# Start addresses of the matmul operands in SBUF, shifted by padding: a hybrid decoder layer on one core

## The chip, the cores and the metric

One core of a Trainium2 chip runs the kernel. The metric is the device time of one execution in microseconds (us); lower is better. A time shown for a kernel is the median of several executions. Beside it stands one profiled execution, whose trace gives the start and the duration of every instruction on every engine.

## The reference

The reference is one layer of a hybrid decoder on 512 positions with a width of 2048, in float32. What matters here is which matrix products it holds:

```
h    = rms_norm(x, norm1_w)
proj = h @ w_in                       # 2048 -> q, k, v (1024 each), z 1024, x/B/C 1536, dt 16
attn = moba_attention(rms(q), rms(k), v)          # 8 heads x 128, causal
ssm  = ssd_chunked_scan(silu(conv4(xBC)), dt, a)  # 16 heads x 64, state 128, gated by silu(z)
x    = x + concat(attn, ssm) @ w_out  # 2048 -> 2048
u    = conv3(rms_norm(x, norm2_w) @ w_up)         # 2048 -> 11264
y    = x + (silu(u_gate) * u_val) @ w_down        # 5632 -> 2048
```

## The kernel before

**Split operands.** A float32 operand `a` is split into `hi` (rounded to the float32r format, on ScalarE) and `lo = a - hi` (on VectorE). A product is then three float32r matmuls: the two with `hi` weights against both parts of the activations, and `lo` weights against the first part. TensorE holds the stationary operand of 128 x 128, which a weight load brings in, and streams the moving operand past it. Both are read from SBUF.

**First stage** (input projection, attention, scan, output projection). All activations lie in 16 tiles `A0..A15` (hi) and 16 tiles `B0..B15` (lo) of [128, 512]. Weights come by DMA into the ring `raw` (3 tiles of [128, 1024]) and are split into the rings `hi` and `lo` (3 tiles of [128, 528] each) by `issue_split`. There are two forms of use. In the feature-major form (`fm_uses`, `wide_use`, through `mm3`) the weights are stationary and `A[k]`, `B[k]` move, 512 columns at a time: `hi.A`, `hi.B`, `lo.A`. In the token-major form (`tok_use`, for v and z) a 128-column slice of `A[k]` or `B[k]` is stationary and the weights move, with 256, 264 or 512 columns. The attention and scan work is done in generators that a planner (`advance`, `Paced`) sets between the pieces when the program is written; the order of the instructions is then fixed. In this stage nearly all instructions carry line 183, the helper's.

**Second stage** (the two products of the gated MLP). Each is done by a seven-product scheme (Strassen-Winograd): 44 `up` groups and 24 `down` groups, each of the products P1 to P7. A product has 8 (in the `down` passes 7, 8 and 7) slices of 128 rows; each slice is one `hi` weight slice against both parts of an activation tile (lines 1286 and 1287), and then all slices of the `lo` weights (line 1289), 256 columns each: 24 matmuls a product, or 21. `items` fixes the order P5(g), P3(g-1), P1(g), P4(g-1), P6(g), P2(g), P7(g). The weights lie in `hi2` (3 tiles) and `lo2` (2 tiles) of [128, 1024], and the activations in seven tiles `cmb0..cmb6` of [128, 2, 8, 256], one for each product:

```
KT1, KT3, K11, KT2, K21, K22, KT4 = range(7)
KIND = {"P5": KT1, "P7": KT3, "P1": K11, "P6": KT2, "P2": K21, "P3": K22, "P4": KT4}
        pool = p2["cmb"] if t < K22 else p2["cmbl"]
```

So P3 streams `cmb5` and P4 `cmb6`, which lie in the left pool `w2`, and the other five stream `cmb0..cmb4`, which lie in a pool at the right end of SBUF.

**Where tiles lie.** Pools on the left are stacked from address 0 of each partition, those on the right from the end. At the left end lie the DMA descriptor scratch (16384 bytes by default), 128 bytes of constants of the framework, and the pool `consts` (5152 bytes), so that the next pool begins at byte 21664. There the pools `w` (`raw`, `hi`, `lo`) and `ab` (`A`, `B`) lie in the first stage, and, once these are closed, the pool `w2` (`par2` 1408 bytes, `rawb`, `rawa`, `acc_s`, `hi2`, `lo2` of 4096 bytes a tile, then `cmb5`, `cmb6`). Summed up, the start addresses modulo 512 bytes are:

| operand | first byte | modulo 512 |
|---|---|---|
| `hi`, three tiles of 2112 bytes | 33952 | 160, 224, 288 |
| `lo`, three tiles of 2112 bytes | 40288 | 352, 416, 480 |
| `A`, `B`, 32 tiles of 2048 bytes | 46624 | 32 |
| `hi2`, `lo2`, five tiles of 4096 bytes | 55840 | 32 |
| `cmb5`, `cmb6` of 16384 bytes | 76320 | 32 |
| `cmb0` to `cmb4` of 16384 bytes | 147424 | 480 |
| attention's `PTh`, `PTl` and `vh`, `vl` (right pool) | 180192 | 480 |

A weight slice of 128 columns has 512 bytes, a moving slice of 256 or 512 columns 1024 or 2048, so all slices of a tile have the same address modulo 512 (but the second slice of the 264-column pieces, which is 32 bytes further).

Of the kernel before, what the change touches and what calls it, by code (L numbers as in the profile page):

```python
# [20 lines left out]
F32 = mybir.dt.float32  # L21
F32R = mybir.dt.float32r
# [165 lines left out]
def body(ctx, tc, xT, wi, wz, wo, wu, wd0, wd1, wd2, pp, pf, outT, dbg={}):  # L188
    nc = tc.nc
# [9 lines left out]
    wpool = ab.enter_context(tc.tile_pool(name="w", bufs=3))  # L199
    abp = ab.enter_context(tc.tile_pool(name="ab", bufs=1))  # L200
# [9 lines left out]


    RW = 1024
    BEHIND = 2.5
    pieces = []

# [14 lines left out]
    def issue_dma(upto):  # L230
        while state["dma"] <= min(upto, len(raw_q) - 1):
            ci = state["dma"]
            src, width = raw_q[ci]
            r = wpool.tile([128, RW], F32, name="raw")
            if ci == 0:
                nc.sync.dma_start(r[:, :512], src[:, :512])
                nc.sync.dma_start(r[:, 512:width], src[:, 512:])
            else:
                nc.sync.dma_start(r[:, :width], src)
            raws[ci] = r  # L240
            state["dma"] += 1

    def issue_split(upto):
        while state["split"] <= min(upto, len(pieces) - 1):
            i = state["split"]
            ci, o, w, _ = pieces[i]
            issue_dma(ci)
            h = wpool.tile([128, 528], F32R, name="hi")
            l = wpool.tile([128, 528], F32R, name="lo")
            src = raws[ci][:, o:o + w]  # L250
            clk["last"] = ("pe", clk["pe"])
            A_.activation(h[:, :w], src, AF.Copy)
            V.tensor_tensor(l[:, :w], src, h[:, :w].bitcast(F32), op=OP.subtract)
            his[i] = (h, l)
            ready[i] = clk["dve"]
            state["split"] += 1

    def dump(n, ap):
        if n in dbg:
            nc.sync.dma_start(dbg[n], ap)  # L260


    A = [abp.tile([128, S], F32R, name=f"A{k}") for k in range(NK)]
    B = [abp.tile([128, S], F32R, name=f"B{k}") for k in range(NK)]
    C = [cpool.tile([128, S], F32, name=f"C{k}") for k in range(NK)]
# [13 lines left out]
    def pc(name, i=0, n=1):  # L279
        o = _PC[name] + i  # L280
        return (p2["par"] if name[0] == "f" else par)[:, o:o + n]
# [54 lines left out]
    def step(e):  # L336
        clk["last"] = ("pe", clk["pe"])
        old = clk["pe"], clk["act"], clk["dve"], clk["pool"]
        e[3] = 0
        try:  # L340
            say = next(e[0])
        except StopIteration:
            if e in gens:
                gens.remove(e)
            return
        if old != (clk["pe"], clk["act"], clk["dve"], clk["pool"]):
            e[1] = max(clk[k] for k in ("pe", "act", "dve", "pool") if k != "pool" or clk[k] != old[3]) + 0.3
        if e not in gens:
            e[2] = e[2] or say == "soon"
            gens.append(e)  # L350
        elif say == "soon":
            e[2] = True
        elif say == "later":
            e[2] = False

    def advance(force=False):

        for e in list(gens):
            e[3] += 1
            ready_ = clk["pe"] >= e[1]  # L360
            if force or (e[2] and (ready_ or e[3] > 1)) or \
                    (ready_ and max(clk["act"], clk["dve"]) < clk["pe"] + BEHIND):
                step(e)
# [308 lines left out]
    def tok_use(k0, nk, cols, box, done):  # L672

        def use(h, l):
# [5 lines left out]
            for kk, t in order:  # L680
# [3 lines left out]
                o = box["acc"][t][:, :cols]  # L684
                T.matmul(o, A[k][:, ts_], h[:, cc], start=k == 0, stop=False)
                T.matmul(o, A[k][:, ts_], l[:, cc], start=False, stop=False)
                T.matmul(o, B[k][:, ts_], h[:, cc], start=False, stop=k == NK - 1)
# [3 lines left out]

    XR = lambda k: (A[k], B[k])

# [8 lines left out]
    def prep_x(k):  # L702
        t = ssq_box[k]
        A_.activation(A[k], t, AF.Copy, scale=pc("nw1", k))
        V.scalar_tensor_tensor(B[k], t, pc("nw1", k), A[k].bitcast(F32), op0=OP.mult, op1=OP.subtract)

# [131 lines left out]
    def split_mix(i):  # L838
# [5 lines left out]
        dump("mix%d" % k, C[k])  # L844
        A_.activation(A[i], C[k], AF.Copy)
        V.tensor_tensor(B[i], C[k], A[i].bitcast(F32), op=OP.subtract)
# [15 lines left out]
    def cmb_tile(t):  # L862

        pool = p2["cmb"] if t < K22 else p2["cmbl"]
        return pool.tile([128, 2, 8, 256], F32R, name="cmb%d" % t)
# [78 lines left out]
    V.memset(u_t[:, 0:3], 0.0)  # L944
    prep_x(0)
    issue_split(0)
    sq_x(0)
    issue_split(1)
    prep_x(1)
    sq_x(1)  # L950
    prep_x(2)
    issue_split(2)
    sq_x(2)
    mix_at = {}
# [15 lines left out]
    lp = ctx.enter_context(tc.tile_pool(name="w2", bufs=1, reuse_waits="tile"))  # L970
# [150 lines left out]
    def x_load(n):  # L1121
        if n < 4:
            x_ld.append(side_tile(box["pool"], [4, 256], "ld", 3))
            sy.dma_start(x_ld[n], xd[:, 4 * (n % 2):4 * (n % 2) + 4, n // 2, :])

    def x_split(n):
        t, h = (K22, KT4)[n // 2], n % 2
        if h == 0:
            up_kinds[t] = cmb_tile(t)
        o = up_kinds[t][:, :, 4 * h:4 * h + 4, :]  # L1130
        se.activation(o[:, 0], x_ld[n], AF.Copy)
        ve.tensor_tensor(o[:, 1], x_ld[n], o[:, 0].bitcast(F32), op=OP.subtract)
        x_load(n + 3)

    for n, slot in enumerate((2, 4, 5, 6)):
        at(slot, x_split, n)
# [135 lines left out]
    for k, (gi, x) in enumerate(items):  # L1272
# [6 lines left out]
        h, l = parts.pop(k)  # L1279
        bk = g["kinds"][KIND[x]]  # L1280
        n = g["n"]
# [36 lines left out]
```

## Time and profile before

| | |
|---|---|
| median of 3 runs | 2115.16 us (2113.25 to 2115.39) |
| profiled execution | 2114.84 us |
| its span, first to last instruction | 2113.1 us |
| TensorE busy | 2073.9 us (98%), 15366 matmuls |
| VectorE busy | 1583.5 us (75%) |
| ScalarE busy | 988.3 us (47%) |
| mean granted TensorE clock | 0.998 of full speed |

The profiled execution's own time is 1.7 us over its span. Engines work in parallel, and busy times overlap. Matmuls are pipelined: one takes 0.28 or 0.39 us from its start to its end, but the next starts before it ends. The number that counts is the spacing from one start to the next, and TensorE can be busy for all of a stretch in which this spacing is longer than it need be.

### The profile page before, as it was taken

Reading aid. Unit: us, or ns where it says so; the run is one execution under the profiler, and the core shown is the slowest. Engines: PE = TensorE matmul, PEld = TensorE weight load, DVE = VectorE, ACT = ScalarE, POOL = GpSimd, SP = SyncE. Lnnn points to the kernel's source line nnn. Section 1 sums busy time; section 2 is a strip of 40 time slices with the busy share of each in tenths; the row PEclk is TensorE's granted clock in tenths of the full one; section 3 lists DMA queues with packets and bytes.
Section 4 is the critical chain, followed back from the end, with each engine's and each line's share of the span. In section 5 each row is a group of like instructions: output and inputs, shape, how many; then the busy total and the mean of one; then the engine's idle time right before and its main releaser. Section 6 shows DMA issues by size and latency. Waiting matters only on the chain.

```text
span 2113.1 us, 37694 instructions
## 1 busy us (share of the span) xinstructions
PE 2073.9 (98%) x15366; PEld 1949.7 (92%) x15366; DVE 1583.5 (75%) x2251; ACT 988.3 (47%) x1433; POOL 207.9 (10%) x107
## 2 busy tenths in 40 slices
PE   9999999999999998999999999999999899999999
PEld 7888887888888878999999999999999899899999
DVE  6545555345555558999999999999999977977976
ACT  5433435244344435555555555555555534534532
POOL 0020000000000001111110111011111111101110
PEclk9999999999999999999999999999999999999999
DMA  5233222332225535445444444454455667856763
GB/s 194 75 115 91 71 75 76 99 101 80 80 70 172 165 129 188 158 141 189 160 156 165 170 168 155 157 183 158 142 188 201 215 215 242 274 184 231 260 201 120
DMA packets 114396, 328.18 MB, mean 155 GB/s; under 512 B 10736, under 2 KB 35120, under 8 KB 111408
## 3 DMA queue, kind: packets, MB, share of 16 engines
q1 hardware_dynamic: 114224, 325.78, 45.5%
q8 instruction: 120, 1.97, 0.4%
q14 instruction: 52, 0.43, 0.1%
HBM read 283.77 MB, written 41.98 MB: 154 GB/s over the span
## 4 chain that ended last, share of the span: by engine, by line
PE 88%; DVE 7%; issue 2%; ACT 1%; DMA 1%; SPq 0%; DVEq 0%; POOL 0%; ACTq 0%; POOLq 0%
PE acc L183 29%; PE x L1289 16%; PE x L1286 16%; PE x L1287 16%; PE sm L183 4%; PE y L1289 3%; PE y L1287 3%; PE y L1286 3%; DVE lo L1050 2%; DVE cmb L1097 1%; DVE lo L183 1%; DVE acc L1151 0%; DVE s L1024 0%; DMA raw<-wi 0%; DVE s L1030 0%
## 5 line engine op out<-in xcount | busy, mean ns | idle before, releaser
L1287 PE MATMUL x<-cmb,hi 128*128 128x256 f32 x3168 | 755.0, 279 | 12.5 <-DVE cmb L1097 10.9
L1286 PE MATMUL x<-cmb,hi 128*128 128x256 f32 x3168 | 755.8, 279 | 11.5 <-ACT cP L1166 5.4
L1287 PEld LDWEIGHTS x<-cmb,hi 128*128 128x128 f32 x3168 | 599.3, 189 | 15.2 <-DVE cmb L1097 13.4
L1286 PEld LDWEIGHTS x<-cmb,hi 128*128 128x128 f32 x3168 | 598.7, 189 | 13.4 <-issue 7.5
L1289 PE MATMUL x<-cmb,lo 128*128 128x256 f32 x3168 | 434.3, 279 | 2.6 <-DVE lo L1050 2.6
L1289 PEld LDWEIGHTS x<-cmb,lo 128*128 128x128 f32 x3168 | 397.2, 189 | 3.6 <-DVE lo L1050 3.4
L183 DVE TENSOR_TENSOR lo<-raw,hi 128x512 fp32r<-128x512 f32 (+1 forms) x240 | 164.4, 691 | 243.0 <-ACT hi L183 228.5
L1041 ACT ACTIVATE hi<-s 128x1024 fp32r<-128x1024 f32 (+1 forms) x201 | 201.0, 1000 | 287.3 <-DVE s L1024 192.2
L1017 POOL TENSOR_TENSOR rawb<-rawa,rawb 128x1024 f32<-128x1024 f32 (+1 forms) x68 | 169.7, 2496 | 1308.1 <-DVE s L1024 1070.8
L183 PE MATMUL acc<-A,hi 128*128 128x512 f32 x704 | 281.5, 400 | 0.5 <-ACT hi L183 0.5
L183 PE MATMUL acc<-A,lo 128*128 128x512 f32 x704 | 277.9, 395 | 0.1
L183 PE MATMUL acc<-B,hi 128*128 128x512 f32 x704 | 276.8, 393 | 0.0
L183 ACT ACTIVATE hi<-raw 128x512 fp32r<-128x512 f32 (+1 forms) x240 | 149.6, 629 | 256.2 <-PE acc L183 220.3
L1050 DVE TENSOR_TENSOR lo<-s,hi 128x1024 fp32r<-128x1024 f32 (+1 forms) x201 | 238.6, 1187 | 18.8 <-issue 18.8
L1050 DVE TENSOR_TENSOR lo<-rawa,hi 128x1024 fp32r<-128x1024 f32 (+1 forms) x204 | 242.0, 1186 | 3.6 <-PE x L1289 3.6
L1041 ACT ACTIVATE hi<-rawa 128x1024 fp32r<-128x1024 f32 (+1 forms) x204 | 209.5, 1028 | 40.0 <-PE x L1287 39.9
L183 PEld LDWEIGHTS acc<-A,lo 128*128 128x128 f32 x704 | 132.1, 188 | 33.0 <-DVE lo L183 2.1
L183 PEld LDWEIGHTS acc<-A,hi 128*128 128x128 f32 x704 | 132.7, 188 | 29.5 <-ACT hi L183 1.8
L183 PEld LDWEIGHTS acc<-B,hi 128*128 128x128 f32 x704 | 132.5, 188 | 28.3
L1166 ACT ACTIVATE cP<-x 128x256 f32<-128x256 f32 x132 | 50.9, 385 | 214.0 <-PE x L1289 214.0
L183 PE MATMUL acc<-hi,A 128*128 128x256 f32 (+2 forms) x448 | 135.4, 302 | 0.7 <-DVE u L183 0.7
L183 PE MATMUL acc<-lo,A 128*128 128x256 f32 (+2 forms) x448 | 133.5, 298 | 0.0
(204 smaller groups left out, 2777.2 us busy)
## 6 DMA issues: line engine op xcount, KB each, us to landing
rawa<-wu SPq DMA_DIRECT2D x176, 512.0 KB, 3.6
raw<-wi SPq DMA_DIRECT2D x79, 512.0 KB, 3.6
rawa<-wd SPq DMA_DIRECT2D x64, 448.0 KB, 4.1
rawb<-wu SPq DMA_DIRECT2D x44, 512.0 KB, 4.5
gd<-gt SPq DMA_DIRECT2D x22, 1024.0 KB, 4.6
raw<-wo SPq DMA_DIRECT2D x32, 512.0 KB, 3.6
rawa<-wd SPq DMA_DIRECT2D x32, 512.0 KB, 4.4
ld<-gd SPq DMA_DIRECT2D x27, 512.0 KB, 6.4
```

The source lines that it names most:

```text
L183: return fn(out, *args, **kw)
L1017: po.tensor_tensor(r, raw[gi, "11"][:, :n], r, op=OP.subtract)
L1041: se.activation(h[:, :n], src[:, :n], AF.Copy)
L1050: ve.tensor_tensor(l[:, :n], src[:, :n], h[:, :n].bitcast(F32), op=OP.subtract)
L1097: ve.tensor_tensor(lo, ld[:, :m, :], hi.bitcast(F32), op=OP.subtract)
L1166: se.activation(g[x], X[:, 256:] if x == "P5" else X[:, :256], AF.Copy)
L1286: pe.matmul(out, w, bk[:, 0, q, :], start=fresh and q == 0, stop=False, skip_group_check=True)
L1287: pe.matmul(out, w, bk[:, 1, q, :], start=False, stop=False, skip_group_check=True)
L1289: pe.matmul(out, l[:, q * 128:(q + 1) * 128], bk[:, 0, q, :], start=False, stop=q == n - 1, skip_group_check=True)
```

## The change

All tiles on the left lie at other addresses. The width of the ring tiles `hi` and `lo` becomes 640 columns (2560 bytes, a multiple of 512). A tile `space` of 112 columns (448 bytes) that nothing reads or writes lies in front of `A0`, and a like one (`space2`) in front of `cmb5`. The descriptor scratch at address 0 shrinks to 1024 bytes, so that everything behind it starts 15360 bytes (30 x 512) lower. No instruction is added, removed or moved, and no operand's shape changes.

```diff
+    WT = 640
...
-            h = wpool.tile([128, 528], F32R, name="hi")
-            l = wpool.tile([128, 528], F32R, name="lo")
+            h = wpool.tile([128, WT], F32R, name="hi")
+            l = wpool.tile([128, WT], F32R, name="lo")
...
+    abp.tile([128, 112], F32, name="space")
     A = [abp.tile([128, S], F32R, name=f"A{k}") for k in range(NK)]
...
     def x_split(n):
         t, h = (K22, KT4)[n // 2], n % 2
+        if n == 0:
+            lp.tile([128, 112], F32, name="space2")
         if h == 0:
             up_kinds[t] = cmb_tile(t)
...
-    nc = _bacc.Bacc("TRN2", target_bir_lowering=False, num_devices=1)
+    nc = _bacc.Bacc("TRN2", target_bir_lowering=False, num_devices=1, dynamic_dma_scratch_size=1024)
```

## Rows read from the trace of the kernel before

**Rows 1.** The page: busy time of each engine, and its share of the span.

```profile
PE 2073.9 (98%) x15366; PEld 1949.7 (92%) x15366; DVE 1583.5 (75%) x2251; ACT 988.3 (47%) x1433; POOL 207.9 (10%) x107
```

**Rows 2.** Waits of TensorE from 790 us: total us, times, longest us.

```profile
PE x L1287 <- DVE cmb L1097: 10.9, 11, 2.3
```

**Rows 3.** Timeline of TensorE: first matmuls of P5, P3, P1, P4, P6, P2.

```profile
1107.37 0.28 PE L1286 MATMUL x<-cmb,hi 128*128 128x256 f32 x1
...
1110.09 0.28 PE L1286 MATMUL x<-cmb,hi 128*128 128x256 f32 x1
...
1112.95 0.29 PE L1286 MATMUL x<-cmb,hi 128*128 128x256 f32 x1
...
1115.69 0.28 PE L1286 MATMUL x<-cmb,hi 128*128 128x256 f32 x1
...
1118.55 0.29 PE L1286 MATMUL x<-cmb,hi 128*128 128x256 f32 x1
...
1121.29 0.28 PE L1286 MATMUL y<-cmb,hi 128*128 128x256 f32 x1
```

**Rows 4.** Windows: TensorE's busy time, matmuls touched, granted clock, DMA share, GB/s.

```profile
660.00:760.00 100.00, 100.00 (x432) 1.00 0.52 164
390.00:420.00 30.00, 30.00 (x132) 1.00 0.30 91
475.00:490.00 15.00, 15.00 (x130) 1.00 0.25 71
1300.00:1600.00 300.00, 300.00 (x2606) 1.00 0.47 167
```

**Rows 5.** Timeline of TensorE in a down group: first matmuls of P3 and P1.

```profile
1945.78 0.28 PE L1286 MATMUL x<-cmb,hi 128*128 128x256 f32 x1
...
1948.64 0.29 PE L1286 MATMUL x<-cmb,hi 128*128 128x256 f32 x1
```

**Rows 6.** Timeline of TensorE in attention: probabilities against values, 256 columns.

```profile
226.33 0.28 PE L183 MATMUL sm<-PTh,vl 128*128 128x256 f32 x1
...
227.05 0.28 PE L183 MATMUL sm<-PTh,vl 128*128 128x256 f32 x1
```

**Rows 7.** Timeline of TensorE: the third and fifth matmul of P1.

```profile
1113.20 0.28 PE L1286 MATMUL x<-cmb,hi 128*128 128x256 f32 x1
...
1113.43 0.28 PE L1286 MATMUL x<-cmb,hi 128*128 128x256 f32 x1
```

**Rows 8.** Timeline of TensorE: one-column matmuls, each behind a full weight load.

```profile
257.75 1.05 PE L183 MATMUL sm<-ones,t 128*128 128x1 f32 x8 [0.94 <-DVE PTl L183]
258.66 0.36 PE L183 MATMUL acc<-hi,A 128*128 128x256 f32 x1
```

**Rows 9.** Timeline of TensorE in the first stage, feature-major: twelve matmuls apart.

```profile
500.31 0.39 PE L183 MATMUL acc<-B,hi 128*128 128x512 f32 x1
...
503.07 0.39 PE L183 MATMUL acc<-B,hi 128*128 128x512 f32 x1
```

**Rows 10.** Groups of TensorE's instructions by line and shape.

```profile
L183 PE MATMUL acc<-A,hi 128*128 128x512 f32 x704 | 281.5, 400 | 0.5 <-ACT hi L183 0.5
L183 PE MATMUL acc<-hi,A 128*128 128x256 f32 x256 | 73.5, 287 | 0.0
```

**Rows 11.** Timeline of TensorE, token-major: third `lo` tile moving, and the next.

```profile
399.68 0.39 PE L183 MATMUL acc<-lo,A 128*128 128x512 f32 x1
399.92 0.39 PE L183 MATMUL acc<-hi,B 128*128 128x512 f32 x1
```

**Rows 12.** Windows over one group, 1104.65 to 1124.01, summed: busy us of each engine.

```profile
sum 19.36, PE 19.36 PEld 19.36 DVE 18.11 ACT 10.06 POOL 2.46; mean PE 2.77 PEld 2.77 DVE 2.59 ACT 1.44 POOL 0.35
```

**Rows 13.** Waits of all engines in the second stage's steady part, 1000:1600.

```profile
DVE lo L1050 <- PE x L1289: 10.4, 16, 0.7
DVE ug L1172 <- PE x L1289: 7.0, 16, 0.4
```

## The prediction

> **What bounds the kernel now.** I read the page first. TensorE is busy for 2073.9 us of a span of 2113.1, and no other engine for more than 75% [rows 1]. Then TensorE's waits: from 790 us on the longest entry is 10.9 us in 11 waits, for activations at the borders of passes [rows 2]. So the time is a count of matmuls times the spacing of their starts, and the next view is the timeline, to find this spacing. It is not one number. In an up group P5, P3, P1, P4, P6 and P2 begin at 1107.37, 1110.09, 1112.95, 1115.69, 1118.55 and 1121.29 us [rows 3]. P5 takes 2.72 us, 113.3 ns for each of 24 matmuls; P3 and P4 take 2.86 us; P1 and P6, which follow those two, 2.74 us. P2 and P7 together have 5.44 of the group's 19.36 us [rows 12], 2.72 each. The shapes and the clock are the same (1.00 in each window, [rows 4]), and TensorE never stops. A down group, with other work on VectorE and the queues, has the same 2.86 us for P3 [rows 5]. So the length goes with the product and not with what else runs. What P3 and P4 have of their own is where their activations lie: 32 bytes modulo 512, which is what `hi2` and `lo2` have, while the other five products have 480.
>
> I call moving start minus stationary start, modulo 512, the offset. It is 448 (that is, -64) for P1, P2, P5, P6, P7 and 0 for P3 and P4. The rows that bear on it: attention's product of probabilities and values has 480 on both sides, offset 0, and its six matmuls from 226.33 to 227.05 stand 120 ns apart [rows 6], which is P3's settled spacing. There the moving operand starts at 480 too, so 480 by itself is not what makes P5 fast; the offset is. And P1's first two spacings are 0.25 us together, the next two 0.23 [rows 3, 7]: a change of offset takes a few matmuls to settle.
>
> How near 113.3 ns is to the floor: eight one-column matmuls, each behind a full weight load, take 0.91 us [rows 8], 114 ns each, the first one's wait included. The 256-column products at offset -64 are as fast as their weight loads.
>
> In the first stage the spacing is 230 ns for 512 columns (2.76 us for twelve, [rows 9]) and 232 over 100 us of the output projection (100.39 us by 432 matmuls, [rows 4]). There `hi` has offsets 384, 320 and 256 and `lo` 192, 128 and 64, so every matmul is followed by one with another offset, and none has -64.
>
> **The change, part by part.** *Descriptor scratch.* 15360 bytes are 30 x 512: by itself this changes no address modulo 512. It makes the room for the rest. All DMAs of this program are started on SP, and no instruction of it reads or writes the scratch: 0 us.
>
> *`space2` in front of `cmb5`.* `w2` begins at 21664 - 15360 = 6304; with `par2` and 13 tiles of 4096 bytes `cmb5` would begin at 60960, with the padding it does at 61408, which is 480 modulo 512. `hi2` (40480) stays at 32. P3 and P4 get the offset -64 of the other five. If they take 2.72 us, P1 and P6 have nothing to settle either, and a group of 24-matmul products loses 2 x 0.14 + 2 x 0.02 = 0.32 us. 44 up and 8 down groups have 24, 16 down groups 21 (three settled matmuls less, 2 x 0.02 us): 52 x 0.32 + 16 x 0.28 = 21.1 us. The other way to count it: 300.28 us hold 2606 matmuls [rows 4], 115.2 ns, and at 113.3 all 11088 would take 21 us less.
>
> *Rings of 640 columns and `space`.* `hi` starts at 18592, `lo` at 26272, each tile 2560 = 5 x 512 bytes long: all six at 160. They end at 33952, `A0` begins at 34400, and all `A`, `B` are at 96. In the feature-major form the offset is now -64 for every matmul. There are three forms of 704, so 2112, of 512 columns [rows 10]. What that gives is not in the trace, since no long run of 512 columns has one offset. [...] I take 222, nearer to 220 because the steady case of P5 is the like one: 9 ns x 2112 = 19 us. One tenth I take off for places where TensorE will wait for attention and scan work: 17 us.
>
> The token-major form gets offset 64 in every matmul: three forms of 256, so 768, of 256 columns [rows 10], and by the plan in the code 384 of 264 and 192 of 512. Now they take about 118 (15.28 us by 130) and 230 (30.39 us by 132) [rows 4]. Nothing shows a steady 64. If it were like -64: 5 x 1152 + 10 x 192 = 8 us gained; if like 0, 2 x 1152 = 2 us lost. I take 0.
>
> *What could take it back.* VectorE has 18.11 us of work in a group of 19.36 [rows 12], and a group would now take 19.04. Its idle time is in part waiting for TensorE, 17.4 us in 600 in the two longest such waits [rows 13], 0.56 us a group by 31 groups, against 0.32 taken away. It stays covered; with no cover at all the group couldn't go under 18.11. The waits on activations at the pass borders [rows 2] are chains of DMA, ScalarE and VectorE; they keep their length.
>
> [...] The trace shows 2.72 and 2.86 us for equal products [rows 3]. [...]
>
> Sum: 2114.8 (the profiled execution; the median is 0.3 higher) - 21.1 - 17 = 2076.7 us.
>
> **The rivals.**
> - *The second stage alone gains.* At 512 columns the weight load is hidden behind the matmul and the slow part has another cause, as the third `lo` tile hints [rows 11]. Then 2114.8 - 21.1 = 2093.7, with the token-major bounds 2086 to 2096. [...]
> - *The offset modulo 512 is not the cause, but the region.* `cmb0..4` lie over 147000, `hi2` under 69000; all slow pairs lie on one side together (`cmb5` and `hi2` low, `PTh` and `vh` high). If the operands must lie in different halves, the change does not do what it says: P3 and P4 stay at 2.86, the first stage stays slow, 2115 give or take 4. Against it: it would have to be halves of the whole memory, for `cmb6`, 24 KB and more behind `hi2`, is no faster than `cmb5`, 8 KB behind it: P3 and P4 are equal [rows 3].
> - *Slower.* One steady offset locks the 512-column matmuls into a bad relation where now good and bad ones mix. To lose, they must cost more than they do now by 21.1 + 4.2 us by 2304 matmuls, 11 ns each, 242 ns. Single spacings of 0.24 us occur [rows 11], longer runs of them do not. At 245 ns: 2114.8 - 21.1 + 14 x 2304 / 1000 = 2126.
>
> **How the numbers follow.** Both stages gain: 0.62, from 2063 (220 ns, nothing lost, the token-major form like -64: 21.1 + 23.2 + 8 = 52 us) to 2087 (227 ns, 8 us). Second stage alone: 0.23. Region, or nothing: 0.11. Slower: 0.04. The predicted time is the first case's, 2077. The range from 2063 to 2096 takes in the second case and leaves out the third and fourth and a little of the tails. A measurement of this kernel can tell about 0.2% from no change. Faster by more: 0.62 + 0.23 and a little of the third, 0.87; within: 0.09; slower: 0.04.
>
> **What would show it.** Right: P3, P4, P1 and P6 at 2.72 us each, a group at 19.04; twelve feature-major matmuls in 2.64 to 2.70 us instead of 2.76; the stretch of the output projection with more than 440 matmuls in 100 us. Wrong: P3 still at 2.86 (region); first stage at 230 (second stage alone); VectorE's `lo` ending TensorE's waits inside the up groups (cover gone). The step I am least sure of is the 222 ns.

## The result, and the profile after

The changed kernel takes 2130.76 us (median of 6 runs, 2128.54 to 2133.87) against 2113.6 (6 runs): a ratio of 1.0081 (95% interval 1.0068 to 1.0094). It is slower by 17 us where 37 us less had been forecast. The profiled execution took 2133.87 us, its span is 2132.2.

The page of the changed kernel, busy times, answers to [rows 1]:

```profile
PE 2093.8 (98%) x15366; PEld 1967.6 (92%) x15366; DVE 1583.5 (74%) x2251; ACT 988.2 (46%) x1433; POOL 207.8 (10%) x107
```

VectorE and ScalarE did the same work in the same time; TensorE's 15366 matmuls take 20 us more. So it is still a matter of spacings. The timeline of the changed kernel, first matmuls of P5, P3, P1, P4, P6 and P2 of one up group [rows 3]:

```profile
1116.43 0.28 PE L1290 MATMUL x<-cmb,hi 128*128 128x256 f32 x1
...
1119.26 0.28 PE L1290 MATMUL x<-cmb,hi 128*128 128x256 f32 x1
...
1122.09 0.28 PE L1290 MATMUL x<-cmb,hi 128*128 128x256 f32 x1
...
1124.91 0.28 PE L1290 MATMUL x<-cmb,hi 128*128 128x256 f32 x1
...
1127.74 0.28 PE L1290 MATMUL x<-cmb,hi 128*128 128x256 f32 x1
...
1130.57 0.28 PE L1290 MATMUL y<-cmb,hi 128*128 128x256 f32 x1
```

All products are alike now, as forecast, but alike at 2.83 us. P3 and P4 fell from 2.86, and P5, whose operands have the same offset as before, rose from 2.72. Windows of the changed kernel over TensorE (busy time, matmuls touched, granted clock, DMA share, GB/s) [rows 4], two of the first stage and three of the second:

```profile
660.00:760.00 100.00, 100.00 (x430) 1.00 0.52 165
390.00:420.00 30.00, 30.00 (x131) 1.00 0.33 104
900.00:1600.00 700.00, 700.00 (x5946) 1.00 0.46 161
1740.00:1800.00 60.00, 60.00 (x531) 1.00 0.69 226
2020.00:2080.00 60.00, 60.00 (x512) 1.00 0.60 200
```

A window also counts the matmul that was running at its start, so the spacing is taken as its length and the 0.28 us of one matmul, by the count: from 900 to 1600 us 700.28 us by 5946, 117.8 ns. From 1740 to 1800 it is 60.28 by 531, 113.5 ns; from 2020 on 117.7 again. The instructions, the addresses modulo 512 and the clock are the same in the three windows. So one offset has two spacings, and the longer one holds here for hundreds of microseconds. Between two of the windows lies a border of a pass. The timeline of the changed kernel there, one wait and the matmuls behind it:

```profile
1995.28 0.28 PE L1290 MATMUL x<-cmb,hi 128*128 128x256 f32 x1
1997.26 0.38 PE L1291 MATMUL x<-cmb,hi 128*128 128x256 f32 x1 [1.70 <-DVE cmb L1099]
...
1997.60 0.28 PE L1291 MATMUL x<-cmb,hi 128*128 128x256 f32 x1
...
1998.78 0.28 PE L1291 MATMUL x<-cmb,hi 128*128 128x256 f32 x1
```

Behind the wait ten spacings take 1.18 us: the spacing of 117.8 ns has begun. Two shorter waits (0.37 and 0.50 us) in the next 15 us turn it to 113.4 ns for about one product and back.

Where the 19 us of span went: the second stage's first matmul starts at 794.34 us in the timeline of the changed kernel and at 791.31 in that of the kernel before. So the first stage lost 3 us and the second 16.

### The profile page after: what moved, and what is told of

It is laid out like the page before. It is cut to its first block, busy times and chain, and to the rows that moved or that the text cites. A ratio compares the mean times of both kernels' runs of the same rounds, so it can differ in the third digit from the quotient of the medians.

```text
span 2132.2 us, 37693 instructions
## 1 busy us (share of the span) xinstructions
PE 2093.8 (98%) x15366; PEld 1967.6 (92%) x15366; DVE 1583.5 (74%) x2251; ACT 988.2 (46%) x1433; POOL 207.8 (10%) x107
## 4 chain that ended last, share of the span: by engine, by line
PE 90%; DVE 7%; issue 1%; DMA 1%; ACT 1%; SPq 0%; DVEq 0%; POOL 0%; ACTq 0%; POOLq 0%
PE acc L183 30%; PE x L1293 16%; PE x L1291 16%; PE x L1290 16%; PE sm L183 4%; PE y L1290 3%; PE y L1293 3%; PE y L1291 3%; DVE lo L1052 2%; DVE cmb L1099 1%; DMA ld<-gd 0%; DVE acc L1155 0%; DVE s L1026 0%; DVE lo L183 0%; DMA acc<-x2d 0%
## 5 line engine op out<-in xcount | busy, mean ns | idle before, releaser
L183 PE MATMUL acc<-hi,B 128*128 128x256 f32 (+2 forms) x448 | 133.4, 298 | 0.0
```

Source lines behind the costliest of these rows:

```text
L183: return fn(out, *args, **kw)
```

## The experiments

**The theory.** At offset -64 the stream of 256-column matmuls holds itself at 113.3 or at 117.8 ns, whichever it fell into, until a gap or matmuls at another offset come. In the kernel before, P3 and P4 at offset 0 set it to 113.3 twice in each group; they cost 0.32 us and saved 0.75. I call it the held spacing (the expectations: latched state). **The rivals:** the shift of all left tiles by 15360 bytes (the expectations: address shift) is what lengthened P5 (the offset modulo 512 is not the whole relation); and, for the first stage, that its spacing has a cause other than the offset.

**The second padding alone.** The kernel before with one edit, so that nothing moves but `cmb5` and `cmb6`:

```diff
+        if n == 0:
+            lp.tile([128, 112], F32, name="space2")
```

> The kernel before with the 448 bytes in front of cmb5 alone (scratch and rings as before, so that no other tile moves but cmb6). Latched state (at offset -64 the spacing holds at 113.3 or at 117.8 ns, whichever it fell into, until another offset or a gap comes; the products at offset 0 had set it back to 113.3 in each group): P3 and P4 lose their 120 ns but all seven products stay at 117.8 from the first group to the first gap of the down passes, so some 44 groups gain 0.43 us each and the rest may be fast: 2113.6 + 18, less up to 8 = 2123 to 2132. Address shift (the 15360 bytes of the scratch set hi2 into a bad relation to cmb0 to cmb4, and the pad is good): all products at 113.3, 2113.6 - 21 = 2092.

Twelve runs from 2095.3 to 2141.2 us, median 2127.5, against 2114.0. They fall into two heaps: five from 2095.3 to 2102.7, seven from 2126.7 to 2141.2, none between. No one ratio describes them, so the times themselves are told here. A kernel whose runs agree within 5 us became one of two times some 30 us apart, and the clock does not part them: the mean granted clock is 0.994 to 0.998 in the lower heap and 0.995 to 0.998 in the upper. The profile is of a run in the upper heap, windows over TensorE:

```profile
840.00:1650.00 810.00, 810.00 (x6879) 1.00 0.46 163
1740.00:1790.00 50.00, 50.00 (x444) 1.00 0.64 210
1860.00:1960.00 100.00, 100.00 (x852) 1.00 0.60 212
```

117.8 ns for 810 us, 113.2 in the first down pass, 117.7 in the second. The scratch had not changed, so the address shift falls, and so does the forecast's own step. The lower heap lies 3 to 11 us above the 2092 that the forecast's own step gives for all runs. That its runs held 113.3 ns is argued, for none of them was profiled: 43 groups at 0.75 us make 32 us, and the medians of the heaps lie 33 apart.

**The scratch alone.**

```diff
-    nc = _bacc.Bacc("TRN2", target_bir_lowering=False, num_devices=1)
+    nc = _bacc.Bacc("TRN2", target_bir_lowering=False, num_devices=1, dynamic_dma_scratch_size=1024)
```

> The kernel before with the small descriptor scratch alone: every left tile lies 15360 bytes lower, with the same addresses modulo 512; no padding, old rings. Latched state and offsets modulo 256: nothing changes, 2113 to 2116, P5 at 2.72 us and P3 at 2.86. Address shift: P5 at 2.83, a group over 20 us, 2140 or more.

2114.68 us against 2113.7, ratio 1.0003 (0.9993 to 1.0013), and 5209 matmuls touched from 1000 to 1600 us as in the kernel before:

```profile
1000.00:1600.00 600.00, 600.00 (x5209) 1.00 0.46 163
```

The shift by itself changes nothing that these runs can tell.

**The change without the second padding.**

```diff
-        if n == 0:
-            lp.tile([128, 112], F32, name="space2")
```

> The changed kernel without the 448 bytes in front of cmb5: the rings, the padding in front of A0 and the small scratch stay. Latched state: P3 and P4 are at offset 0 again and set the others back to 113.3, a group takes 19.36 us as before, and only the first stage changes: 233.5 instead of 231.5 ns on 2304 matmuls, 4 to 5 us, so 2117 to 2119. Address shift: hi2 lies where it lies in the changed kernel, so P5, P7, P1, P6, P2 stay at 117.8 and P3, P4 at 120: a group takes 20 us, 2113.6 + 40 = 2154.

2116.11 us, ratio 1.001 (1.0002 to 1.0019): 2 us of the loss are the first stage's, and with P3 and P4 back at offset 0 the second stage is that of before. Windows over TensorE, with 5209 by 600 us there too:

```profile
1000.00:1600.00 600.00, 600.00 (x5209) 1.00 0.46 163
660.00:760.00 100.00, 100.00 (x430) 1.00 0.52 166
```

Its first stage has the same addresses as that of the changed kernel, and still one piece differs. z's token-major piece, 512 columns at a steady offset of 64, windows over TensorE of the changed kernel and of this run:

```profile
385.00:425.00 40.00, 40.00 (x173) 1.00 0.30 92
385.00:425.00 40.00, 40.00 (x177) 1.00 0.31 92
```

From start to start these are 233 and 229 ns, 0.8 us by its 192 matmuls: at 512 columns, too, one offset can have two spacings.

**One product left to set the spacing.** The kernel before with the padding between `cmb5` and `cmb6`: P3 stays at offset 0, P4 gets -64.

```diff
+        if n == 2:
+            lp.tile([128, 112], F32, name="space2")
```

> The kernel before with the 448 bytes in front of cmb6 instead of cmb5: P3 stays at offset 0, P4 gets -64. Latched state: one product in each group sets the state back, which is enough, so P4 takes 2.72 us and P6 too, a group 19.20 instead of 19.36: 68 groups, 2113.6 - 10.5 = 2103. If both resets are needed in each group: some products at 117.8, 2113 or more. Address shift: 2103 as well, since no scratch changes.

2104.09 us, 5 runs from 2103.1 to 2106.9, ratio 0.9957 (0.9945 to 0.9969): forecast 2103. One reset a group keeps the other six products at 113.3 ns, P4 among them: 600.28 us by 5253 matmuls is 114.3 on the mean.

```profile
1000.00:1600.00 600.00, 600.00 (x5253) 1.00 0.46 163
```

**A reset by hand.** The second padding alone, and twelve matmuls more in the whole kernel, whose output the next matmul overwrites:

```diff
+    KICK = (3,)
...
+        if x == "P5" and gi in KICK:
+            for q in range(12):
+                w = h[:, q % 8 * 128:(q % 8 + 1) * 128]
+                pe.matmul(out, w, h[:, :256], start=True, stop=True, skip_group_check=True)
```

> As the run with the padding in front of cmb5 alone, and 12 extra matmuls of 256 columns at offset 0 (the hi2 tile against itself, their output overwritten by the next matmul) in front of P5 of the fourth up group. Latched state: these 12 set the state to 113.3 and it holds with no further help through some 40 up groups, until a gap: a group takes 19.04 us from there on, 2113.6 - 0.32 x 40 + 1.4 for the extra matmuls, and the down passes as luck has it: 2090 to 2105. If the state does not hold by itself: 2125 to 2133, as without the extra matmuls. Address shift: 2094.

2098.62 us, 6 runs from 2096.6 to 2107.4, ratio 0.9938 (0.9921 to 0.9954). No run lies in the upper heap; two, of 2105.6 and 2107.4, lie above the lower one. Windows over TensorE, ahead of the twelve matmuls, and behind them:

```profile
810.00:860.00 50.00, 50.00 (x428) 1.00 0.41 148
900.00:1600.00 700.00, 700.00 (x6179) 1.00 0.47 166
2020.00:2080.00 60.00, 60.00 (x532) 1.00 0.52 172
```

50.28 us by 428 is 117.5 ns, 700.28 by 6179 is 113.3: twelve matmuls, 1.4 us, took over 4 ns from each of the 6179 in that window alone. This is the experiment that settles that a stream holds its spacing and that a short disturbance changes it, for nothing else differs from the run with two heaps, and both spacings stand in one execution.

**How many it takes.** The whole changed kernel, with `KICK = {4: 1, 8: 2, 12: 3, 16: 4, 20: 6, 24: 8, 28: 12}`, up group to number of extra matmuls, and `range(KICK[gi])`.

> The whole changed kernel with extra matmuls at offset 0 in front of P5 of up group 4 (one of them), 8 (two), 12 (three), 16 (four), 20 (six), 24 (eight) and 28 (twelve); their output is overwritten. Latched state: all groups are at 117.8 ns until the first of these sets that is long enough, and at 113.3 from there on to the next gap. P3's transient at offset 0 in the kernel before lasted 8 matmuls, so the switch is expected at group 24 or 20: some 20 groups gain 0.75 us, 2131 - 15 = 2116, less what the down passes give. If a single matmul at another offset is enough, the switch is at group 4 and the time 2131 - 30 = 2101. If the state does not hold with this first stage, no switch and 2135.

2111.02 us in one run beside 2113.83 for the kernel before. Windows over TensorE, ahead of group 4, behind it, behind group 8, behind 16 and behind 20:

```profile
850.00:880.00 30.00, 30.00 (x257) 1.00 0.36 124
900.00:940.00 40.00, 40.00 (x342) 1.00 0.46 167
970.00:1110.00 140.00, 140.00 (x1238) 1.00 0.44 156
1120.00:1190.00 70.00, 70.00 (x597) 1.00 0.41 141
1200.00:1600.00 400.00, 400.00 (x3530) 1.00 0.46 164
```

The spacings are 117.8, 117.8, 113.3, 117.7 and 113.4 ns. One extra matmul left the 117.8 as it was; two ended it (I had expected six or eight); three left the 113.3 as it was; four ended it; six ended the 117.8, and eight and twelve were followed by 113.3 again. So it is no threshold, as far as one case of each shows: a disturbance sets the spacing anew, to either side. Whole products at offset 0, 21 or 24 matmuls, are steadier: in the five traces that have them, all 554 products at -64 that follow one without a wait settle at 113.3. And in the eleven traces of this document other than the scan's no stream at -64 changes from one spacing to the other by itself: between the two stands a wait (the shortest a start 0.03 us late), matmuls at offset 0, or other work of TensorE.

**Many offsets in one run.** The changed kernel with paddings that give each `A[k]`, `B[k]` the offset 64 x k to the rings, and each product of the second stage another offset:

```diff
+    def apart(name):
+        abp.tile([128, 16], F32, name="pad" + name)
+        return abp.tile([128, S], F32R, name=name)
...
+        for t, gap in ((KT1, 384), (KT3, 256), (K11, 128), (KT2, 64), (K21, 64)):
             p2["kinds"][t] = cmb_tile(t)
+            p2["cmb"].tile([128, gap // 4], F32, name="gap%d" % t)
...
+        if n in (0, 2):
+            lp.tile([128, 32], F32, name="gap%d" % n)
```

> The changed kernel with other paddings, so that one run shows many offsets: in the first stage 64 bytes more between the A tiles and between the B tiles, which gives A[k] and B[k] the offset 64 x k modulo 512 to the rings in the feature-major form; in the second stage P5, P3, P1, P4, P6, P2, P7 get the offsets 64, 128, 192, 256, 320, 384, 448. If one fixed offset is good for 512 columns, the twelve matmuls of a k in the wide form and of its like have 220 to 226 ns at some k and 231 to 240 at the others; if the spacing at 512 columns has another cause, all k are within 2 ns of 232. In the second stage: if offset -64 alone has the fast state, the other six settle at 117 to 120 and P7 at 113 or 118; if the fast state is there at most offsets once something resets it, most are at 113. No statement on the total time by either.

One run, 2138.36 us. Timeline of TensorE in an up group, first matmuls of P1 (offset 192), P4 (256), P6 (320), P2 (384), P7 (448), P5 (64), P3 (128) and the next P1:

```profile
1197.55 0.28 PE L1295 MATMUL x<-cmb,hi 128*128 128x256 f32 x1
...
1200.29 0.28 PE L1295 MATMUL x<-cmb,hi 128*128 128x256 f32 x1
...
1203.15 0.28 PE L1295 MATMUL x<-cmb,hi 128*128 128x256 f32 x1
...
1205.98 0.28 PE L1295 MATMUL y<-cmb,hi 128*128 128x256 f32 x1
...
1208.83 0.28 PE L1295 MATMUL x<-cmb,hi 128*128 128x256 f32 x1
...
1211.65 0.28 PE L1295 MATMUL x<-cmb,hi 128*128 128x256 f32 x1
...
1214.48 0.28 PE L1295 MATMUL x<-cmb,hi 128*128 128x256 f32 x1
...
1217.33 0.28 PE L1295 MATMUL x<-cmb,hi 128*128 128x256 f32 x1
```

P1 at 192 takes 2.74 us, settling included; P4 at 256 takes 2.86, like P3 at 0 in the kernel before [rows 3]; 320 and 64 take 2.83, 384 and 128 take 2.85. P7 at 448 had the longer spacing here (2.82). So the relation repeats after 256 bytes at the offsets measured, not only after 512, and of the four offsets modulo 256 only 192 shows 113.3. In the first and third down pass, where a product has 21 matmuls, P7 and P1 change places; first matmuls of P7, P5, P1 and P4 there:

```profile
1766.54 0.28 PE L1295 MATMUL x<-cmb,hi 128*128 128x256 f32 x1
...
1768.93 0.28 PE L1295 MATMUL x<-cmb,hi 128*128 128x256 f32 x1
...
1773.88 0.28 PE L1295 MATMUL x<-cmb,hi 128*128 128x256 f32 x1
...
1776.36 0.28 PE L1295 MATMUL x<-cmb,hi 128*128 128x256 f32 x1
```

P7 takes 2.39 us for 21 matmuls, 113.8 ns with what settles, and P1 2.48, 118.1 ns. Both offsets can have either spacing, and in this run the number of matmuls ahead goes with which one it is, in all groups without a wait. In the first stage the same run has, for twelve matmuls of one k in the wide form, first matmuls of k = 10, 11, 12 and 13:

```profile
35.07 0.39 PE L183 MATMUL acc<-A,hi 128*128 128x512 f32 x1
...
37.85 0.40 PE L183 MATMUL acc<-A,hi 128*128 128x512 f32 x1
...
40.66 0.39 PE L183 MATMUL acc<-A,hi 128*128 128x512 f32 x1
...
43.42 0.40 PE L183 MATMUL acc<-A,hi 128*128 128x512 f32 x1
```

k = 10 (offset 128) takes 2.78 us, k = 11 (192) 2.81, k = 12 (256) 2.76; k = 9 and 13 (64 modulo 256) take 2.76, too. For 512 columns 192 modulo 256 is the worst of the four, and 0 and 64 are the best: the other way round than for 256 columns. It lies within the 2 ns of 232 for most k, though, so a steady case was wanted.

**The first stage at offset 0.** The changed kernel without either padding: `A0` right behind the rings.

```diff
-    abp.tile([128, 112], F32, name="space")
...
-        if n == 0:
-            lp.tile([128, 112], F32, name="space2")
```

> The changed kernel without both paddings of 448 bytes: rings of 640 columns and A0 right behind them, so that the feature-major form has offset 0 in every matmul instead of -64; P3 and P4 are at offset 0 as before. Theory that the offset modulo 256 sets the spacing at 512 columns (the scan: 227 at 0, 233 at 192): 227 to 228 instead of 231.5 on 2112 matmuls, minus 8 us, and the token-major form, also at offset 0, loses up to 2: 2113.8 - 6 = 2107 to 2109. Theory that the first stage has another limit and the scan's differences are of the moment: 2113 to 2117, as with the padding in front of A0.

2107.11 us, 5 runs from 2105.8 to 2107.6, ratio 0.9966 (0.9954 to 0.9979). Windows over TensorE in the output projection and in z's token-major piece:

```profile
655.00:755.00 100.00, 100.00 (x443) 1.00 0.55 172
390.00:415.00 25.00, 25.00 (x112) 1.00 0.35 106
```

100.39 us by 443 is 226.6 ns; it was 232.4 [rows 4] and 233.5 in the changed kernel. z's piece went from 230 [rows 4] to 226.7.

**Resets at the borders of the passes, and all together.** `KICK = (3, 46, 54, 62)` on the kernel with the second padding alone, with `q % n` in place of `q % 8`, since a weight tile has 7 or 8 slices there:

> The kernel before with the 448 bytes in front of cmb5 and the extra matmuls in front of P5 of the groups 3, 46, 54 and 62; the first stage is that of before. Latched state: as with the extra matmuls in front of group 3 alone, 2097 to 2100, but no run at 2105 and more, since a pass that falls into the 117.8 ns state at its border is set back in its third group. If what spread the runs was something else than the state: the same spread of 11 us.

2100.89 us, 5 runs from 2100.0 to 2104.3, ratio 0.9941 (0.9929 to 0.9954). The runs spread over 4 us instead of 11, but the median is 1 us over the range given: what the three more resets cost was not made up. The same resets with the first stage at offset 0:

> The same first stage (offset 0), the 448 bytes in front of cmb5, and 12 extra matmuls at offset 0 in front of P5 of the groups 3 (up), 46, 54 and 62 (one in each down pass). Latched state and offset modulo 256 together: first stage minus 6, second stage minus 0.32 x 66 plus 4 x 1.4 us: 2113.8 - 6 - 21 + 6 = 2093, 2088 to 2098, all runs within some 5 us since the state is set again behind each border. If the first stage gains nothing: 2099.

2093.52 us, 4 runs from 2092.7 to 2097.6, ratio 0.9901 (0.9886 to 0.9917), where 2093 had been expected: 21 us under the kernel before and 37 under the changed one. The resets do not make a pass sure, though. The profiled execution is the longest of the four, and its first down pass did not hold 113.3. Windows over TensorE behind group 46, with the resets alone and with the first stage at offset 0, too:

```profile
1740.00:1790.00 50.00, 50.00 (x444) 1.00 0.80 266
1740.00:1790.00 50.00, 49.97 (x424) 1.00 0.78 255
```

The first is 113.2 ns; the second 118.6, a short wait included. In the second trace the twelve matmuls of group 46 were followed by 113.3, but waits of 0.6 and 1.2 us and a start 0.2 us late came behind them, and behind the last the products take 117.8 until the end of the pass.

## Why the prediction was wrong

*The second stage, -21.1 us, came out as +16.* P3 and P4 did "get the offset -64 of the other five", and they lost their 120 ns. The step that failed is the next one, "If they take 2.72 us", and with it "480 by itself is not what makes P5 fast; the offset is": that a product's spacing follows from its offset alone, so that P3 and P4 would take P5's 2.72 us and P5 keep them. All seven took 2.83. What had not been seen is that P3 and P4 also were the reason why the other five ran at 113.3. The sum with the measured spacings: a group of 168 matmuls takes 19.36 us with the two resets, 19.04 at 113.3 ns without them, and 168 x 117.8 ns = 19.79 at the other spacing. From about 820 to 1670 us 43 groups lose 0.43 us each, 18 us; the down passes, the first two of which held 113.3 for the most part, gave 2 back.

The trace of the kernel before shows it, in a place that the prediction does not use. The P5 of its second group runs ahead of the first P3, behind the waits at the start of the stage; the timeline of the kernel before has there

```profile
816.61 0.28 PE L1286 MATMUL x<-cmb,hi 128*128 128x256 f32 x1
...
818.14 0.28 PE L1287 MATMUL x<-cmb,hi 128*128 128x256 f32 x1
```

and thirteen spacings in 1.53 us are 117.7 ns, at the offset that takes 113.3 in every later up group. And P1's first spacings after P3 were read as settling [rows 3, 7], which already said that a spacing depends on what went before.

*The first stage, -17 us, came out as +3.* The step "I take 222, nearer to 220 because the steady case of P5 is the like one" failed: what is good for 256 columns was bad for 512. A steady -64 takes 233.5 ns, 1.1 more than the 232.4 of the mixture of offsets before, where the gain of both stages had been counted with 220 to 227. The 220 and the 222 are spacings that no run shows: the lowest over a long stretch of 512 columns was 226.6 ns, at offset 0. The rival "Slower" had this place and this kind of mechanism, but at 242 ns, and kept the second stage's gain; that the time is near its 2126 is chance.

*What held.* The token-major form was put at 0: its 512-column piece has 131 matmuls touched in 30 us against 132, under 1 us in all. VectorE stayed covered: in the run with twelve extra matmuls TensorE is busy for all of the 700 us at 113.3 ns. The changed kernel itself could not show this, for its groups were longer. The region rival falls: with the second padding alone only `cmb5` and `cmb6` moved, by 448 bytes and on their own side, and the products with `cmb0` to `cmb4` changed their spacing too; and in the scan P3, near `hi2`, and P2, far from it, take the same 2.85 us at offsets that are the same modulo 256.

*What stays open.* In the runs above the same 256-column matmuls take 113.3, 117.8 or 120 ns at a granted clock of 1.00, by start addresses and by what went before. What holds the spacing inside TensorE or SBUF is not shown. Nor is it shown that the extra matmuls had to be at another offset: none were added at the stream's own, and waits change the spacing, too. Nor why the six runs of the changed kernel, by their times, all began at 117.8, while five of twelve with the second padding alone began at 113.3; the only difference there is the first stage and the 15360 bytes.

## What to carry to other kernels

When equal instructions have different durations, ask what the longer ones do to those behind them before making them like the shorter: do it to one of them first, as the run with the padding in front of `cmb6` did, and look at the neighbours. A kernel that streams long runs of matmuls with all operands at one offset can have several times for one program, as the one with the second padding alone did (2095 to 2141 us); look at all the runs, not at the median, and at the spacing by windows. Offsets of moving to stationary operand are worth a scan for each column count, since 192 modulo 256, the best for 256 columns (113.3 ns), was among the worst for 512 (233.5 ns).

## What the runs showed of the hardware that was not expected

- A stream of 256-column float32r matmuls at offset 192 modulo 256 holds at 113.3 or 117.8 ns; the spacing lasted over 700 us and more than 6000 matmuls, and in the traces it changed only behind matmuls at another offset (two were enough once), other work, or a wait.
- At offset 0 modulo 256 such matmuls take 120 ns; at 512 columns the same offset is the best seen (226.6 ns), 192 takes 233.5, and 64 took 233 in the changed kernel and 229 in the run without its second padding.
- 448 bytes of padding split one kernel's runs into two heaps, with the median 13 us higher (2127.5), and twelve matmuls of no use brought it to 2098.6.
